# A mixer stage whose TensorE sequence is written by a timing model: other costs and rules in the model, and the other engines' order left to the framework's scheduler

## The chip, the core and the metric

The kernel runs on one NeuronCore of one Trainium2 chip. The metric is the device time of one execution in microseconds (us). TensorE (PE) multiplies matrices and writes to PSUM; VectorE (DVE) and ScalarE (ACT) do the elementwise work, GpSimd (POOL) a little more of it, and SyncE (SP) issues the loads. Each engine works through its own list of instructions in that list's order, and waits where an instruction needs what another engine has not finished.

## The reference, cut to what matters

One encoder layer: a feed-forward block (ffn), a mixer, a second ffn. All numbers are float32, with 512 tokens and 16 learned tokens ahead of them (T = 528), model width 1024.

```python
h = h + 0.5 * swiglu(rms_norm(h, ffn1_norm), ...)
u = rms_norm(h, mix_norm)
z = u @ w_in
zq_a, zi_a, zf_f, zf_b, zg_a, zq_b, zk_b, zv_b, zgate_a, zgate_b = split_cols(z, IN_SIZES)
y_a = hgrn2_bidir(zq_a, zi_a, zf_f, zf_b, zg_a, ...)    # 4 heads, a gated recurrence in both directions
y_b = axial_gqa(zq_b, zk_b, zv_b, ...)                  # 8 heads of softmax attention, 2 key heads
mixed = sigmoid(zgate_a) * (y_a @ w_up_a) + sigmoid(zgate_b) * (y_b @ w_up_b)
h = h + mixed @ w_out
h = h + 0.5 * swiglu(rms_norm(h, ffn2_norm), ...)
```

## The kernel before, in words

Every product of a weight with an activation is made of three matmuls, since both sides are cut into a high and a low part: whi with xh, whi with xl, wlo with xh. A weight block arrives in `raw` by DMA; ACT casts it to `whi`, DVE subtracts to get `wlo`. One block of 128 output rows is 8 slices of 3 matmuls; over 512 tokens each is one matmul of 512 columns, over 528 tokens it is one of 256 and one of 272.

The two ffns are scheduled by the framework and are not touched. The mixer is ordered by the program itself, in class `Order` (line 161 on). It holds a clock `t` for PE, times at which DVE and ACT come free, and a list of chains, each a Python generator with the time `ready` at which its next step could start. The main chain issues the weight products (`zcols`); after every slice of three matmuls `tick` calls `pump`, which runs the steps of all chains whose time has come. `account` charges each recorded instruction to the model: a matmul to `t`, a DVE or ACT instruction to that engine. `need` runs chains until a condition holds; where nothing is ready it moves `t` forward. `take` and `give` hand out the three PSUM banks named mm. So PE's list is what the model thinks will be ready when PE gets there. In the program before, a `manual_schedule` over ACT, DVE and POOL (line 699) binds these three to the order in which the model recorded their instructions too; PE is bound by an outer one (line 625).

The chains: `gla` (the recurrence of head hd) first makes a diagonal product, `gs<-zi,ks` on PE. Then come seven levels: ACT copies `ks` out of Z, PE makes four products `gs<-Z,ks`, DVE multiplies Z and tot (`grow`) and copies by mask from gs into A; an eighth product is `gs<-Z`. `gla_finish` transposes, makes the state (`vt,on`, `vt,st`) and the output (`vt,A`, `st,Z`), normalises it (ACT squares, twelve tiny DVE instructions in `newton`, ACT scales into `on`), and transposes on PE (`mm<-ident,on`). `scores` runs one attention tile at a time: four matmuls into S, a maximum on DVE (`nm`), `nr` and the exponential `pr` on ACT, a reciprocal `sm` on DVE, and a scaling of `pr` on ACT. `turned` transposes `pr` on PE (into at and am), ACT casts to `ph`, DVE subtracts to `pl`, and after four tiles PE multiplies with the values (`ph,vs`). There are 32 tiles in four groups j. The gates (`gate`, seven of them ahead of the attention's end, an eighth at c = 5) are weight products whose sigmoids ACT takes after the attention. Exp and sigmoid need different tables on ACT, and a change between them puts an ACT_TABLE_LOAD ahead.

`Timed` wraps the engines so that every recorded instruction carries the line of its one call, line 276; in the mixer, groups are told apart by their tiles.

Of the kernel before, what the change touches and what calls it, by code (L numbers as in the profile page):

```python
# [15 lines left out]
P = 128  # L16
D = 1024
KT = D // P
# [142 lines left out]
class Order:  # L161
# [12 lines left out]
    def account(self, eng, op, args, kw):  # L174
        out = kw.get("out", args[0])
        n, cur = 1, self.cur
        for d in out.shape[1:]:
            n *= d
        if eng == "pe":
            if cur is not self.main:  # L180
                self.t = max(self.t, cur.ready)
            if op == "transpose":
                self.t += 0.11
            elif args[1].dtype == F32R:
                self.t += n / 2400 + 0.0133
            else:
                self.t += max(4 * n / 2400, 0.06) + 0.005
            cur.ready, cur.eng = self.t + self.DRAIN, eng
            return
        if eng == "act":  # L190
            d = n * 0.000916 + 0.115
            if "accum_out" in kw:
                d += 0.19
            f = args[2] if len(args) > 2 else kw.get("func")
            if f in (AF.Exp, AF.Sigmoid, AF.Sqrt) and f != self.table:
                self.table = f
                d += 1.28
        elif op == "reciprocal":
            d = 0.0065 * n + 0.12
        elif op == "tensor_reduce":  # L200
            d = 0.70
        elif op == "memset":
            d = 0.15
        else:
            d = (n + 160) / 960
        start = max(self.free.get(eng, 0.0), cur.ready + (self.HOP if cur.eng != eng else 0.0))
        self.free[eng] = cur.ready = start + d
        cur.eng = eng
# [4 lines left out]
    def ready(self, ch):  # L213
        return ch.ready if ch.wait is None or ch.wait() else float("inf")

# [64 lines left out]
def block_kernel(tc, xT, wg1, wu1, wd1, w_in, wup, wout, wg2, wu2, wd2, params,  # L280
# [18 lines left out]
    with (tc.tile_pool(name="persist", bufs=1) as sp, tc.tile_pool(name="wts", bufs=1) as wp,  # L299
# [271 lines left out]
        with tc.tile_pool(name="f1", bufs=1) as ft:  # L571
# [45 lines left out]
            plan += tiles[:EARLY] + tiles[KT:KT + 5] + tiles[EARLY:KT] + tiles[KT + 5:]  # L617
            for c in range(KT):
# [6 lines left out]
        with tc.tile_pool(name="mix", bufs=1) as mp, tc.manual_schedule(engines={pe.engine}):  # L625
# [22 lines left out]
            def weights():  # L648
# [5 lines left out]
                if not W.ready:  # L654
# [42 lines left out]
            YA = []  # L697
            with (tc.tile_pool(name="heads", bufs=1) as hp, tc.tile_pool(name="small", bufs=1) as mn,
                  tc.manual_schedule(engines={act.engine, dve.engine, pool.engine})):
                Timed.clock = il  # L700
# [136 lines left out]

                waiting = []
                out_of = [0]

                def scores():

                    for j in range(HEADS):
# [3 lines left out]
                        for e in range(2):  # L847
                            for c in range(4):
# [27 lines left out]
                def turned():  # L876

                    for j in range(HEADS):
                        yb.append(mp.tile([P, SEQ], F32, name="yb", tag="yb", bufs=4))
                        for e in range(2):  # L880
# [3 lines left out]
                            for c in range(4):  # L884
                                yield lambda: waiting
                                _, _, _, pr, ready = waiting.pop(0)
                                il.cur.ready = max(il.cur.ready, ready)
# [16 lines left out]
                                yield  # L904
                            yield lambda: il.banks and out_of[0] < 3
                            av, v = mm(), VS[j // 2]
# [45 lines left out]
                def gla_inputs(hd):  # L952
# [5 lines left out]
                    scaled(Z[:, 3], zcols(SEQ))  # L958
                    yield
                    if hd:  # L960
# [3 lines left out]
                    yield  # L964
                    scaled(Z[:, 0], zcols(T))
                    yield
# [22 lines left out]
                def gla_head(hd, Z, tot, q, v):  # L989

                    A = hp.tile([P, 2, 4, P], F32, name="A", tag="A", bufs=2)
                    vt = hp.tile([P, 5, P], F32, name="vt", tag="vt", bufs=2)
                    ks = kbuf()
                    dve.tensor_tensor(ks, Z[:, 0, :SEQ], Z[:, 3, :SEQ], ALU.add)
                    first = il.cur.ready
                    o = four()
# [81 lines left out]
                def gla_out(hd, Z, tot, A, vt):  # L1078
# [59 lines left out]
                    give()  # L1138

                for gen in (prepare(), scores(), turned(), gla(), gla_finish()):  # L1140
                    il.add(gen)
                queries(0)
                gi = gla_inputs(0)
                kz, ksq = tmp("keys"), tmp("keys")
                scaled(kz, zcols(T))
# [14 lines left out]
                def gate(sg):  # L1160
                    (o, _), = zcols(SEQ)
                    dve.tensor_tensor(sg, o, R[:, :SEQ], ALU.mult)
                    give()

# [5 lines left out]

                sgs = []
                for c in range(EARLY):
                    sg = mp.tile([P, SEQ], F32, name="mixb", tag="mb", bufs=4) if c < 4 else tmp(f"b{c}")[:, :SEQ]
                    gate(sg)
                    sgs.append(sg)
# [3 lines left out]
                ybl = hp.tile([P, 4, SEQ], F32R, name="ybl", tag="pl")  # L1179
                for j, y in enumerate(yb):  # L1180
                    split((ybh[:, j, :], ybl[:, j, :]), y, slice(0, SEQ))
                    YB.append((ybh[:, j, :], ybl[:, j, :]))
                for sg in sgs:
                    act.activation(sg, sg, AF.Sigmoid)

                mixb = []
                for c in range(KT):
                    if c == 5:
                        sgs.append(tmp()[:, :SEQ])
                        gate(sgs[-1])  # L1190
                        act.activation(sgs[-1], sgs[-1], AF.Sigmoid)
# [117 lines left out]
```

## Time and profile before

| | us |
|---|---|
| time, median of 3 runs (lowest, highest) | 1239.66 (1239.02, 1242.03) |
| the profiled execution: its own time | 1241.96 |
| its span | 1240.1 |
| PE busy in the span | 1185.0 |
| DVE busy | 870.3 |
| ACT busy | 577.1 |
| POOL busy | 100.0 |

The stretch of the mixer that the change touches lies between about 381 and 752 us of the span. The page cuts the span into 40 slices of 31 us; PE falls below nine tenths in the first, the last, and slices 14 to 16 and 18 to 21 counted from 0, all in that stretch. A matmul in the trace lasts longer than the distance to the next one's start, since they are pipelined: a run of them costs its starts' distance.

### The profile page before, as it was taken

How to read it: one execution, taken by the hardware profiler on the slowest of the kernel's cores; microseconds unless marked ns; L12 is line 12 of the kernel's file. 1: busy time of each engine (PE TensorE's matmuls, PEld its weight loads, DVE VectorE, ACT ScalarE, POOL GpSimd, SP SyncE). 2: the span in 40 equal slices, each digit the busy share in tenths (PEclk: the TensorE clock that was granted, in tenths of full speed). 3: DMA queues.
4: the chain of work that ended last, by engine and by line, in shares of the span. 5: the costliest groups of instructions: out<-in, count | busy, mean ns of one | idle time of the engine just before them, and what ended most of it. 6: DMA issues, size and time to landing. Idle time of an engine off the chain costs nothing. (4 is left out here: it accounts for less than half of the span.)

```text
span 1240.1 us, 19340 instructions
## 1 busy us (share of the span) xinstructions
PE 1185.0 (96%) x7765; PEld 1077.0 (87%) x7765; DVE 870.3 (70%) x1409; ACT 577.1 (47%) x979; POOL 100.0 (8%) x77
## 2 busy tenths in 40 slices
PE   8999999999999987898888999999999999999998
PEld 8999999999998965786776887888888998998997
DVE  7988658748757786477686765545598875875863
ACT  5545435425554555545736424333454543543541
POOL 1011000001021000000000000112200201101100
PEclk8999999999999998899999999999999999999999
DMA  6233333322132210021020112323422423323213
GB/s 225 61 109 120 91 97 107 99 86 103 45 97 99 86 35 17 18 68 52 18 69 18 52 60 70 109 88 117 136 85 86 136 86 102 119 86 102 103 52 119
DMA packets 34233, 106.21 MB, mean 86 GB/s; under 512 B 3936, under 2 KB 4320, under 8 KB 34144
## 3 DMA queue, kind: packets, MB, share of 16 engines
q1 hardware_dynamic: 33984, 104.44, 26.1%
q8 instruction: 61, 1.00, 0.3%
q0 software_dynamic: 160, 0.54, 0.1%
q14 instruction: 28, 0.23, 0.1%
HBM read 102.87 MB, written 2.10 MB: 85 GB/s over the span
## 5 line engine op out<-in xcount | busy, mean ns | idle before, releaser
L101 ACT CAST whi<-raw 128x1024 fp32r<-128x1024 f32 (+2 forms) x179 | 150.0, 839 | 251.7 <-PE mm L294 88.6
L102 DVE TENSOR_TENSOR wlo<-raw,whi 128x1024 fp32r<-128x1024 f32 (+2 forms) x179 | 177.6, 995 | 20.6 <-ACT whi L101 18.6
L276 PE MATMUL mm<-xh,whi 128*128 128x512 f32 (+1 forms) x352 | 115.5, 365 | 0.0
L276 PE MATMUL mm<-xl,whi 128*128 128x512 f32 (+1 forms) x352 | 109.2, 348 | 0.0
L276 PE MATMUL mm<-xh,wlo 128*128 128x512 f32 (+1 forms) x352 | 109.0, 347 | 0.0
L102 DVE TENSOR_TENSOR wlo<-sums,whi 128x1024 fp32r<-128x1024 f32 x72 | 87.5, 1217 | 25.0 <-ACT whi L101 24.8
L101 ACT CAST whi<-sums 128x1024 fp32r<-128x1024 f32 x72 | 75.4, 1050 | 62.4 <-DVE sums L128 20.9
L133 POOL TENSOR_TENSOR sums<-raw 128x512 f32<-128x512 f32 x36 | 58.8, 1634 | 492.6 <-DVE wlo L102 483.4
L276 PEld LDWEIGHTS mm<-xh,wlo 128*128 128x128 f32 x352 | 62.3, 192 | 8.2
L276 PEld LDWEIGHTS mm<-xh,whi 128*128 128x128 f32 x352 | 62.9, 193 | 7.3 <-issue 0.7
L276 PEld LDWEIGHTS mm<-xl,whi 128*128 128x128 f32 x352 | 62.7, 193 | 5.4
L294 PE MATMUL mm<-hh,wlo 128*128 128x256 f32 (+1 forms) x218 | 63.0, 334 | 0.0
L294 PE MATMUL mm<-hh,whi 128*128 128x256 f32 (+1 forms) x218 | 62.8, 333 | 0.1
L294 PE MATMUL mm<-hl,whi 128*128 128x256 f32 (+1 forms) x218 | 62.9, 332 | 0.0
L471 PE MATMUL mm<-xl,whi 128*128 128x264 f32 (+1 forms) x216 | 61.3, 284 | 0.0
L471 PE MATMUL mm<-xh,whi 128*128 128x264 f32 (+1 forms) x216 | 61.2, 283 | 0.0
L471 PE MATMUL mm<-xh,wlo 128*128 128x264 f32 (+1 forms) x216 | 61.1, 283 | 0.0
L276 ACT CAST whi<-raw 128x1024 fp32r<-128x1024 f32 (+1 forms) x41 | 39.4, 965 | 36.9 <-PE mm L276 27.8
L294 PE MATMUL mm<-xh,whi 128*128 128x512 f32 (+2 forms) x152 | 51.4, 365 | 2.7 <-ACT xh L375 2.7
L276 DVE TENSOR_TENSOR wlo<-raw,whi 128x1024 fp32r<-128x1024 f32 (+1 forms) x41 | 45.8, 1116 | 9.8 <-ACT whi L276 9.6
L294 PE MATMUL mm<-xl,whi 128*128 128x512 f32 (+2 forms) x152 | 51.8, 367 | 0.0
L294 PE MATMUL mm<-xh,wlo 128*128 128x512 f32 (+2 forms) x152 | 51.2, 363 | 0.0
(351 smaller groups left out, 3574.3 us busy)
## 6 DMA issues: line engine op xcount, KB each, us to landing
raw<-in_wg SPq DMA_DIRECT2D x43, 512.0 KB, 3.9
raw<-in_wu SPq DMA_DIRECT2D x43, 512.0 KB, 3.3
raw<-in_w_in SPq DMA_DIRECT2D x42, 512.0 KB, 3.3
raw<-in_wd SPq DMA_DIRECT2D x48, 384.0 KB, 3.1
raw<-in_wd SPq DMA_DIRECT2D x16, 256.0 KB, 2.7
raw<-in_wup SPq DMA_DIRECT2D x16, 256.0 KB, 2.7
raw<-in_wout SPq DMA_DIRECT2D x8, 512.0 KB, 3.3
h<-in_xT SPq DMA_DIRECT2D x4, 528.0 KB, 6.7
```

Of the source, the lines that this page charges most:

```text
L101: nc.scalar.copy(hi[:, c], src)
L102: nc.vector.tensor_tensor(lo[:, c], src, hi[:, c].bitcast(F32), ALU.subtract)
L133: nc.gpsimd.tensor_tensor(t[:, E], r0[:, E], r1[:, E], ALU.add)
L276: return f(*args, **kw)
L294: pe.matmul(o, a[:, sl], b[:, cols], start=(k == 0 and i == 0), stop=(k == n - 1 and i == 2))
L471: pe.matmul(o, a[:, sl], b[:, kk, :], start=(start and kk == 0 and i == 0), stop=(kk == 3 and i == 2), skip_group_check=True)
```

## The change

The model: a chain's step on PE no longer waits for the drain of the chain's own PE step before it; an activation with `accum_out` costs 0.20 and not 0.19, one with a scale taken from a tile 0.17 more; a DVE `tensor_scalar` of over 64 columns costs (n + 160) / 1400 and not / 960. A condition may now give a time from which it holds, and `has_bank` gives the time at which a bank comes free; where the main chain wants a bank, other chains' steps due before that time are run first, and the clock moves with them.

The chains: the end of a softmax tile (reciprocal and scaling) is a chain of its own, so that `scores` goes on to the next tile; Z's forward gate is projected ahead of the query; two gates move into the loop over heads; the keys' squares take a buffer from `pr`'s set; the next weight's cast is recorded at once; sigmoids of the gates are recorded each behind its branch. The scheduling: ACT, DVE and POOL are no longer bound in the mixer. The framework's scheduler orders them by what it thinks is ready, with PE's list given.

```diff
         if eng == "pe":
-            if cur is not self.main:
+            if cur is not self.main and cur.eng != eng:
                 self.t = max(self.t, cur.ready)
...
             if "accum_out" in kw:
-                d += 0.19
+                d += 0.2
+            if not isinstance(kw.get("scale", 1.0), (int, float)):
+                d += 0.17
...
+        elif op == "tensor_scalar" and n > 64:
+            d = (n + 160) / 1400
         else:
             d = (n + 160) / 960
...
     def ready(self, ch):
-        return ch.ready if ch.wait is None or ch.wait() else float("inf")
+        w = True if ch.wait is None else ch.wait()
+        return max(ch.ready, 0.0 if w is True else w) if w else float("inf")
...
     def has_bank(self):
-        return bool(self.banks)
+
+        return self.banks and min(self.banks) + 1e-6
 
     def take(self):
 
         if self.cur is self.main:
-            self.need(self.has_bank)
+            while not self.banks or min(self.banks) > self.t:
+                ch = min(self.chains, key=self.ready, default=None)
+                r = self.ready(ch) if ch else float("inf")
+                if self.banks and min(self.banks) <= r:
+                    break
+                assert r < float("inf"), "nothing can go on"
+                self.t = max(self.t, r)
+                self.step(ch)
         r = min(self.banks)
...
-            order = [Z_QB, Z_KB, Z_FB, Z_VB, Z_QA, Z_FF, Z_G, Z_I]
+            order = [Z_QB, Z_KB, Z_FB, Z_VB, Z_FF, Z_QA, Z_G, Z_I]
             for hd in range(1, HEADS):
-                order += [c + hd for c in (Z_QB, Z_FB, Z_QA, Z_FF, Z_G, Z_I)]
+                order += [Z_GB + hd - 2] if hd > 1 else []
+                order += [c + hd for c in (Z_QB, Z_FB, Z_FF, Z_QA, Z_G, Z_I)]
...
-                    il.need(lambda: not W.ahead_raw)
+                    il.step(il.chains[-1])
                     W.fetch()
...
-            with (tc.tile_pool(name="heads", bufs=1) as hp, tc.tile_pool(name="small", bufs=1) as mn,
-                  tc.manual_schedule(engines={act.engine, dve.engine, pool.engine})):
+            with tc.tile_pool(name="heads", bufs=1) as hp, tc.tile_pool(name="small", bufs=1) as mn:
...
+                def scaled_rows(i, pr, sm):
+                    yield
+                    dve.reciprocal(sm, sm)
+                    yield
+                    act.activation(pr, pr, AF.Copy, scale=sm)
+                    pending[i] = pr, il.cur.ready
...
                                 act.activation(pr, s[:, WIDE], AF.Exp, bias=nr, scale=r, accum_out=sm)
-                                yield
-                                dve.reciprocal(sm, sm)
-                                yield
-                                act.activation(pr, pr, AF.Copy, scale=sm)
-                                waiting.append((j, e, c, pr, il.cur.ready))
+                                il.add(scaled_rows(len(pending), pr, sm))
+                                pending.append(None)
...
                 for hd in range(1, HEADS):
                     if hd > 1:
+                        early(hd - 2)
                         il.need(lambda: f"att{hd - 2}" in il.done)
...
-                for sg in sgs:
-                    act.activation(sg, sg, AF.Sigmoid)
...
                     b = branch(YB)
+                    act.activation(sgs[c], sgs[c], AF.Sigmoid)
```

The first place is on PE, behind the first head's output product. `ident,on` is the transposition of the normalised head; `at` and `am` are transpositions of a softmax tile, S the next tile's scores, `xh,whi` a weight product. Before:

```order
L276 MATMUL at<-ident,pr 128x128 x4
L276 MATMUL am<-ident,pr 16x128
L276 MATMUL mm<-xh,whi 128x256
L276 MATMUL mm<-xh,whi 128x272
L276 MATMUL mm<-xl,whi 128x256
L276 MATMUL mm<-xl,whi 128x272
L276 MATMUL mm<-xh,wlo 128x256
L276 MATMUL mm<-xh,wlo 128x272
L276 MATMUL mm<-ident,on 128x128 x4
```

A slice of weight product stood ahead of `ident,on`. Now, at the same place of PE's list:

```order
L289 MATMUL at<-ident,pr 128x128 x4
L289 MATMUL am<-ident,pr 16x128
L289 MATMUL S<-kh_4805,qst 128x256
L289 MATMUL S<-kh_4805,qst 128x272
L289 MATMUL S<-kl_4806,qst 128x256
L289 MATMUL S<-kl_4806,qst 128x272
L289 MATMUL mm<-ident,on 128x128 x4
L289 MATMUL mm<-kones,tq 128x2 x4
L289 MATMUL mm<-xh,whi 128x512
```

Four score matmuls stand directly ahead of it, and no weight product.

The second place is on ACT, at the start of the second group of attention tiles, with their exponentials `pr,sm<-S`. `mixb` is a gate's tile, and its row the sigmoid. The gates' sigmoids before, all behind the attention:

```order
L276 ACTIVATE on,ss<-mm 128x128 x4
L276 CAST ybh<-yb 128x512 x4
L276 ACTIVATE mixb<-mixb 128x512 x4
L276 ACTIVATE tm<-tm 128x512 x3
L276 ACTIVATE on<-mm,yo 128x128 x4
```

They stood together, with no table load between them. Now the first of them:

```order
L289 ACTIVATE pr<-pr,sm 128x528
L289 COPY vt<-gs 16x128
L289 ACT_TABLE_LOAD
L289 ACTIVATE mixb<-mixb 128x512
L289 COPY on<-mm 128x512
L289 ACTIVATE nr<-nm,yq 128x1
L289 COPY ks<-Z 128x512
L289 ACT_TABLE_LOAD
L289 ACTIVATE pr,sm<-S,nr,yq 128x528
L289 COPY st<-mm 128x128 x2
L289 ACTIVATE pr<-pr,sm 128x528
L289 CAST ph<-at 128x4x128
```

One sigmoid has moved between two exponentials and brought two table loads with it. Over the whole program ACT's list has 30 loads where it had 14.

The third place is on PE, in the second group of attention tiles: what stands between one tile's scores S and the transpositions of the tile ahead. Before:

```order
L276 MATMUL S<-kh_4766,qst 128x256
L276 MATMUL S<-kh_4766,qst 128x272
L276 MATMUL S<-kl_4767,qst 128x256
L276 MATMUL S<-kl_4767,qst 128x272
L276 MATMUL mm<-xh,whi 128x256
L276 MATMUL mm<-xh,whi 128x272
L276 MATMUL mm<-xl,whi 128x256
L276 MATMUL mm<-xl,whi 128x272
L276 MATMUL mm<-xh,wlo 128x256
L276 MATMUL mm<-xh,wlo 128x272
L276 MATMUL at<-ident,pr 128x128 x4
L276 MATMUL am<-ident,pr 16x128
```

Now the transpositions and the next scores, in the order of the list:

```order
L289 MATMUL at<-ident,pr 128x128 x4
L289 MATMUL am<-ident,pr 16x128
L289 MATMUL mm<-xh,whi 128x256
L289 MATMUL mm<-xh,whi 128x272
L289 MATMUL mm<-xl,whi 128x256
L289 MATMUL mm<-xl,whi 128x272
L289 MATMUL mm<-xh,wlo 128x256
L289 MATMUL mm<-xh,wlo 128x272
L289 MATMUL S<-kh_4805,qst 128x256
L289 MATMUL S<-kh_4805,qst 128x272
L289 MATMUL S<-kl_4806,qst 128x256
L289 MATMUL S<-kl_4806,qst 128x272
```

Six weight matmuls have moved from behind S to ahead of it, and behind this S stand 24 more weight matmuls, a level's product and one more slice until the next transpositions.

## Rows read from the trace of the kernel before

**Rows 1.** The page: the span, part 1's engines, and the granted clock of PE in 40 slices, in tenths.

```profile
span 1240.1 us, 19340 instructions
...
PE 1185.0 (96%) x7765; PEld 1077.0 (87%) x7765; DVE 870.3 (70%) x1409; ACT 577.1 (47%) x979; POOL 100.0 (8%) x77
...
PEclk8999999999999998899999999999999999999999
```

**Rows 2.** Busy time by stretch of the mixer: from the first to the last level product of a head, then on to the next head's first, for the four heads, and all of it. Columns: stretch, its length, then busy us and instructions of PE, PE's weight loads, DVE, ACT, POOL; PE's granted clock, DMA share, GB/s.

```profile
438.30:482.80 44.50, 32.47 (x181) 26.50 (x181) 37.15 (x72) 23.94 (x45) 0.00 (x0) 0.92 0.08 24
482.80:543.90 61.10, 53.19 (x305) 44.51 (x306) 31.98 (x67) 34.71 (x73) 0.18 (x2) 0.92 0.09 28
543.90:580.10 36.20, 31.30 (x194) 27.00 (x194) 31.28 (x58) 13.30 (x19) 0.00 (x0) 1.00 0.19 66
580.10:620.80 40.70, 34.59 (x221) 28.80 (x222) 25.38 (x57) 28.65 (x64) 0.44 (x2) 1.00 0.06 21
620.80:657.00 36.20, 31.24 (x194) 26.98 (x193) 31.29 (x58) 13.30 (x19) 0.00 (x0) 1.00 0.19 66
657.00:698.50 41.50, 35.97 (x221) 30.25 (x222) 25.47 (x57) 28.64 (x64) 0.42 (x1) 0.96 0.06 20
698.50:730.90 32.40, 32.24 (x171) 27.23 (x170) 24.81 (x35) 8.55 (x11) 0.00 (x0) 1.00 0.20 71
730.90:752.10 21.20, 20.05 (x112) 16.63 (x111) 9.99 (x25) 11.43 (x31) 0.00 (x0) 1.00 0.08 26
438.30:752.10 313.80, 271.06 (x1593) 227.88 (x1594) 217.34 (x426) 162.52 (x326) 1.04 (x5) 0.97 0.12 38
```

**Rows 3.** PE's waits between 420 and 800 us, the four longest in total: what waited, for which tile of which engine, us in total, times, the longest.

```profile
PE gs L276 <- DVE A L276: 17.1, 15, 3.7
PE at L276 <- DVE pl L276: 6.6, 6, 1.8
PE mm L276 <- ACT on L276: 4.0, 2, 2.0
PE at L276 <- ACT pr L276: 3.1, 6, 0.7
```

**Rows 4.** PE in order of time: start, length, instruction. The distance of two starts is what the first costs.

```profile
424.79 0.40 PE L276 MATMUL S<-kh,qst 128*128 128x256 f32 x2
...
425.28 0.40 PE L276 MATMUL mm<-xh,whi 128*128 128x256 f32 x2
...
431.12 0.39 PE L276 MATMUL mm<-xh,whi 128*128 128x512 f32 x1
431.35 0.39 PE L276 MATMUL mm<-xl,whi 128*128 128x512 f32 x1
...
435.48 0.60 PE L276 MATMUL at<-ident,pr 128*128 128x128 f32 x4
...
436.02 0.27 PE L276 MATMUL gs<-ident,tm 128*16 128x128 f32 x1
...
438.30 1.16 PE L276 MATMUL gs<-zi,ks 128*128 128x128 f32 x8 [0.62 <-ACT vt L276]
439.21 0.49 PE L276 MATMUL S<-kh,qst 128*128 128x256 f32 x2
```

**Rows 5.** PE in order of time: the scores of three attention tiles that follow one another.

```profile
492.60 0.75 PE L276 MATMUL S<-kh,qst 128*128 128x256 f32 x2
...
497.24 0.79 PE L276 MATMUL S<-kh,qst 128*128 128x256 f32 x2
...
502.44 0.49 PE L276 MATMUL S<-kh,qst 128*128 128x256 f32 x2
```

**Rows 6.** Groups of instructions of DVE and ACT between 400 and 780 us, shapes apart: count, busy us, mean ns of one, idle time before them.

```profile
L276 DVE TENSOR_REDUCE nm<-S 128x1 f32<-128x528 f32 x32 | 22.3, 698 | 1.0 <-PE S L276 0.7
L276 DVE TENSOR_TENSOR pl<-at,ph 128x512 fp32r<-128x512 f32 x32 | 22.0, 687 | 13.9 <-ACT ph L276 13.9
...
L276 DVE SCALAR_TENSOR_TENSOR ao<-ao,xo 128x4 f32<-128x4 f32 x12 | 2.0, 163 | 0.4
L276 DVE TENSOR_SCALAR Z<-Z,oml 128x512 f32<-128x512 f32 x4 | 1.9, 487 | 0.1
...
L276 ACT ACTIVATE pr<-pr,sm 128x528 f32<-128x528 f32 x32 | 23.6, 736 | 3.8 <-DVE sm L276 3.8
...
L276 ACT ACT_TABLE_LOAD x8 | 10.3, 1283 | 0.2
L276 ACT ACTIVATE nr<-nm,yq 128x1 f32<-128x1 f32 x32 | 9.5, 296 | 39.5 <-DVE nm L276 39.1
...
L276 ACT ACTIVATE on<-mm,yo 128x128 f32<-128x128 f32 x16 | 4.6, 370 | 4.2 <-DVE yo L276 4.2
...
L276 ACT ACTIVATE mixb<-mixb 128x512 f32<-128x512 f32 x4 | 2.2, 640 | 0.0
```

**Rows 7.** ACT in order of time around one table load, with the exponential behind it.

```profile
428.95 0.29 ACT L276 ACTIVATE nr<-nm,yq 128x1 f32<-128x1 f32 x1
429.26 1.28 ACT L276 ACT_TABLE_LOAD   x1
430.55 0.79 ACT L276 ACTIVATE pr<-S,nr,yq 128x528 f32<-128x528 f32 x1
```

**Rows 8.** Busy time by stretch, columns as in Rows 2: the 20 us in which the granted clock was lowest.

```profile
480.00:500.00 20.00, 16.96 (x86) 13.42 (x85) 10.36 (x21) 11.55 (x27) 0.00 (x0) 0.83 0.00 1
```

More of the change, by code (lines that the diff above doesn't have):

```diff
@@ L610, in last1 @@
                     rstd([(bank(g)[:, :c.stop - c.start], c) for g, c in zip(("gs", "at"), FULL)], T)
-            order = [Z_QB, Z_KB, Z_FB, Z_VB, Z_QA, Z_FF, Z_G, Z_I]
+            order = [Z_QB, Z_KB, Z_FB, Z_VB, Z_FF, Z_QA, Z_G, Z_I]
             for hd in range(1, HEADS):
-                order += [c + hd for c in (Z_QB, Z_FB, Z_QA, Z_FF, Z_G, Z_I)]
+                order += [Z_GB + hd - 2] if hd > 1 else []
+                order += [c + hd for c in (Z_QB, Z_FB, Z_FF, Z_QA, Z_G, Z_I)]
             plan = [w_in[c] for c in order]
             tiles = [w_in[Z_GB + c] for c in range(KT)] + [wup[c][:, 512:] for c in range(KT)]
-            plan += tiles[:EARLY] + tiles[KT:KT + 5] + tiles[EARLY:KT] + tiles[KT + 5:]
+            plan += tiles[HEADS - 2:EARLY] + tiles[KT:KT + 5] + tiles[EARLY:KT] + tiles[KT + 5:]
             for c in range(KT):
@@ L836, in prepare @@
                         yield from queries_rest(j, arg)
-                waiting = []
+                pending = []
                 out_of = [0]
+                def scaled_rows(i, pr, sm):
[4 more added lines that the diff above has]
+                    pending[i] = pr, il.cur.ready
                 def scores():
@@ L884, in turned @@
                             for c in range(4):
-                                yield lambda: waiting
-                                _, _, _, pr, ready = waiting.pop(0)
+                                i = (2 * j + e) * 4 + c
+                                yield lambda: len(pending) > i and pending[i] is not None
+                                pr, ready = pending[i]
                                 il.cur.ready = max(il.cur.ready, ready)
@@ L904, in turned @@
                                 yield
-                            yield lambda: il.banks and out_of[0] < 3
+                            yield lambda: out_of[0] < 3 and il.has_bank()
                             av, v = mm(), VS[j // 2]
@@ L959, in gla_inputs @@
                     yield
+                    scaled(Z[:, 0], zcols(T))
+                    yield
                     if hd:
@@ L963, in gla_inputs @@
                     scaled(zi[:, 0], zcols(SEQ))
-                    yield
-                    scaled(Z[:, 0], zcols(T))
                     yield
@@ L993, in gla_head @@
                     ks = kbuf()
+                    ready = il.cur.ready
                     dve.tensor_tensor(ks, Z[:, 0, :SEQ], Z[:, 3, :SEQ], ALU.add)
-                    first = il.cur.ready
+                    first, il.cur.ready = il.cur.ready, ready
+                    yield
                     o = four()
@@ L1138, in gla_out, with gate, early @@
                     give()
+                def gate(sg):
+                    (o, _), = zcols(SEQ)
+                    dve.tensor_tensor(sg, o, R[:, :SEQ], ALU.mult)
+                    give()
+                sgs = []
+                def early(c):
+                    sg = mp.tile([P, SEQ], F32, name="mixb", tag="mb", bufs=4) if c < 4 else tmp(f"b{c}")[:, :SEQ]
+                    gate(sg)
+                    sgs.append(sg)
                 for gen in (prepare(), scores(), turned(), gla(), gla_finish()):
@@ L1143, in block_kernel @@
                 gi = gla_inputs(0)
-                kz, ksq = tmp("keys"), tmp("keys")
+                kz, ksq = tmp("keys"), hp.tile([P, TP], F32, name="ksq", tag="pr", bufs=3)[:, :T]
                 scaled(kz, zcols(T))
@@ L1158, in block_kernel @@
                         pass
[L1160 to L1163, printed above, removed]
                 def branch(y):
@@ L1169, in branch @@
                     return b
[L1171 to L1175, printed above, removed]
+                for c in range(HEADS - 2, EARLY):
+                    early(c)
                 il.need(lambda: "attention" in il.done)
@@ L1179, in block_kernel @@
                 ybl = hp.tile([P, 4, SEQ], F32R, name="ybl", tag="pl")
+                ready = il.t
                 for j, y in enumerate(yb):
+                    il.main.ready = ready
                     split((ybh[:, j, :], ybl[:, j, :]), y, slice(0, SEQ))
                     YB.append((ybh[:, j, :], ybl[:, j, :]))
-                for sg in sgs:
-                    act.activation(sg, sg, AF.Sigmoid)
                 mixb = []
@@ L1190, in block_kernel @@
                         gate(sgs[-1])
-                        act.activation(sgs[-1], sgs[-1], AF.Sigmoid)
                     b = branch(YB)
+                    act.activation(sgs[c], sgs[c], AF.Sigmoid)
                     m = sgs[c] if c < 4 else mp.tile([P, SEQ], F32, name="mixb", tag="yb", bufs=4)
```

## The prediction

> **What bounds the kernel now.** I read the page first [rows 1]: PE is busy 1185.0 of 1240.1 us, so 55.1 us of PE are idle, and the granted clock is below nine tenths only in the first slice and in the middle of the span. Then the table by stretch [rows 2]. There the reader is to see three things. PE is idle for 313.8 - 271.06 = 42.7 us between 438.3 and 752.1. In the first head's levels, where DVE works 37.15 of 44.5 us, PE works least; in the fourth's, where attention is over, PE has 32.24 of 32.40. And in the levels of heads two and three DVE is busy 31.28 of 36.2 us, 86%, though it is DVE and its chain that hold PE there: 86% is as full as DVE gets. Third, PE's waits [rows 3]: 17.1 us are level products waiting for DVE's A, 6.6 and 3.1 us transpositions waiting for a softmax tile, 4.0 us the head's output. None of the four is for a DMA.
>
> Busy time hides a part of the loss, since a matmul behind a wait or at half clock shows as longer. So I count PE's list by the distance of starts [rows 4]: 0.23 us for a matmul of 512 columns, 0.24 for a pair of 256 and 272 (24 pairs from 425.28 to 431.12), 0.49 for a tile's four scores, 0.54 for a tile's five transpositions, 0.91 for a level's product. From the first head's `gs<-zi,ks` to the last `ident,on` the list of before has 447 weight matmuls of 512 columns (102.1 us at 0.2285), 288 halves (35.1), 30 tiles of scores (14.7) and 31 of transpositions (16.8), 36 level products (31.7 at 0.88), 72 matmuls of values (16.9, as long as weight matmuls), and 139 small ones (23.5, at 0.17 between a transposition's 0.11 and a level product's 0.22): 240.8 us. It took 313.8. The loss is 73.0 us, 42.7 of it shown as idle and the rest as slow clock and refilling. By the stretches of rows 2 the counted work is 25.0, 44.8, 28.6, 31.6, 28.6, 31.6, 31.0 and 19.8 us, so the losses are 19.5, 16.3, 7.6, 9.1, 7.6, 9.9, 1.4 and 1.4. A better placed list can give back that sum and no more; the ffns are untouched.
>
> **The change part by part.** *The costs.* The corrected costs meet the trace [rows 6]: `tensor_scalar` of 512 columns took 487 ns, where the model had (512 + 160) / 960 = 0.70 us and now has 0.48; the tiny `nr` took 296 ns, where it had 0.12 and now has 0.29; the scaling of `pr` took 736 ns, where it had 0.60 and now has 0.77. They lengthen a tile's chain in the model by 0.34 us; I give them nothing of their own, since they act through the list.
>
> *The list of PE.* It has 250.2 us of work from the first `gs<-zi,ks` to the last `ident,on`: all matmuls are as many as before, but the stretch now holds 36 more weight matmuls of 512 columns (8.2 us, gates and branch products that stood behind it) and one tile each more of scores and transpositions (1.0). What moves is the spacing. PE's work from the first to the last level product of a head was 25.0, 28.6, 28.6 and 31.0 us; it is now 49.0, 48.4, 42.7 and 39.2. The DVE work in such a run was 37 us in the first head and 31 in the next two [rows 2], that is 149% and 109% of PE's, and 80% in the fourth; the losses were 19.5, 7.6, 7.6 and 1.4. The same DVE work, 217 us and about 5 for what came in, now lies along 250 us of PE work, at 89%. Between 80% and 109% I read the loss off the straight line: 1.4 + 6.2 x 9/29 = 3.3 us for a run of 36 us, and there are seven such lengths in 250 us: 23 us. DVE alone bounds the stretch from below by 222 / 0.86 = 258 us, a loss of 8.
>
> Between the level runs PE lost 16.3, 9.1 and 9.9 us because attention tiles came one behind the other: their scores start 4.6 and 5.2 us apart [rows 5], which is the chain of maximum, `nr`, exponential, reciprocal, scaling and transposition with too little between them. Now the 31 tiles spread over all 250 us, one in 8, and a tile's tail no longer holds the next one's scores in the model. That removes this wait; what is late next is the queue of ACT and DVE.
>
> *What the scheduler's order adds.* Three kinds of place carry a wait that the model did not see. Directly ahead of the first head's `ident,on` stand a tile's scores. On DVE the twelve `newton` instructions of that head are now spread among others, and the last of them lie behind the maximum of just that tile; on ACT the scaling into `on` stands behind that tile's exponential and the scaling of the tile before. From the scores' end [rows 6]: maximum 0.70, `pl` 0.69, six tiny ones 1.1, the scaling of `pr` 0.74, the four scalings into `on` about 1.2 (they overlap; one is 0.37): 4.4 us less 0.3 that PE's four transpositions take, a wait of 4.1. Queued behind it on PE is everything else, a level product first. Two tiles' scores stand behind a table load: a copy of about 0.6 (an estimate from the sigmoid on as many columns, 0.64), the load 1.28 and the exponential 0.79 [rows 6, 7] make 2.7 us where PE has 1.6 and 1.3 of work: 2.5 us together. At the end the last tile's values follow its transposition at once: some 1 us. Sum 7.6; nothing, if a backlog elsewhere covers them.
>
> *Table loads.* ACT's list has 30 loads where it had 14: eight times a sigmoid now breaks a row of exponentials. At 1283 ns each [rows 6] that is 20.5 us more on ACT. ACT was busy 162.5 of 313.8 us [rows 2]; with the loads it is 183 of 282, 65%, and a tile's exponential has 8 us to happen in. I take them as hidden but for the two places above; if none is, 18 us more come on top. A load costs ACT its own length here: it starts 0.02 us after `nr` ends, and the exponential 0.01 us after the load [rows 7]. The Trainium skill (ScalarE: Activation LUTs, What ACT_TABLE_LOAD costs) states 1283 ns for the load, as rows 6 have it, and 1380 ns of drain with every switch, which rows 7 do not show. By that page sixteen switches would be 42.6 us on ACT, and with none hidden but the two above my sum would come out at 1239.
>
> *Weights and loads.* The next weights' cast and subtraction stay one block ahead, the loads on SP are as many and in nearly the same order, and no wait for `wlo` is among PE's longest [rows 3]. I cost them at nothing; the cover is one block of 24 x 0.23 = 5.5 us, and without it a block's cast and subtraction would be paid.
>
> The sum: 23 + 7.6 + 1.4 (the end as before) = 32 us lost where 73 were. The profiled execution took 1241.96 us, 1.9 more than its span: 1242.0 - 73.0 + 32.0 = 1201.0. It lies 2.3 us above the median of the runs, so I predict 1198.7, rounded 1199. The ends: a loss of 16 (DVE's floor of 8 and the places) gives 1183; a loss of 32 + 18, and 20 more for places that I priced at nothing, gives 1237.
>
> **The rivals.** *Smaller gain, the loads on the path.* The eight broken rows of exponentials delay a tile that PE's list wants at once. For it: the model gives a step to PE as soon as it thinks it ready, with a slice of 0.7 us as slack. Against it: one tile in 8 us, with a chain of 4.6. Price 18 to 38 us: 1217 to 1237.
>
> *The change doesn't do what it says: order against order.* PE's list is made by one model, the others' by a scheduler with another, and where the two differ a list waits as it did. The 4.1 us at `ident,on` are such a case. All of the 73 us would have to come back: 1240. Against it: of four `ident,on` only the first stands so.
>
> *Slower: ACT becomes the late engine.* The place is ACT's queue, where a pair of loads and a sigmoid (2 x 1.283 + 0.64 = 3.2 us) stand ahead of an exponential. If each of the eight stops PE in full, that is 26 us, and each stop may lower the clock: from 480 to 500 us the granted clock was 0.83 [rows 8], 17% of 20 = 3.4 us lost, eight times 27. With the 32 that makes 85 us, more than 73: 1242.0 - 73.0 + 85 - 2.3 = 1252. It decides once the losses pass 73, that is 41 us beyond my terms. If the Trainium skill's drain were paid as well, the losses would pass it sooner; the rows show no drain.
>
> *Larger gain.* If the straight line is too harsh and 89% on DVE costs as little as 80% did (1.4 us a run, 10 in all) and a backlog covers the places, 1242.0 - 73.0 + 11 - 2.3 = 1178.
>
> **How the numbers follow.** My forecast, 1185 to 1217: 0.58. Smaller gain, 1217 to 1236: 0.20. Larger, below 1185: 0.07. The same, 1236 to 1243: 0.05. Slower: 0.10. A measurement of this kernel can tell 0.3%, 3.7 us, from no change. So faster 0.84 (the first three, less 0.01 at the border), same 0.06, slower 0.10. The range 1183 to 1238 leaves out 0.06 below and 0.14 above; the likeliest case alone is 1185 to 1217.
>
> **What would show it.** In the changed profile PE's waits for A fall from 17.1 to under 8 us, those for `pl` and `pr` together from 9.7 to under 6, and PE's busy share passes 97%. The stretch from the first `gs<-zi,ks` to the last `ident,on` takes about 282 us, with the clock at 0.98 or more and DVE near 78%. One wait of 3 to 5 us for `on` stands in the first head. Table loads are 30, and ACT's busy time grows by 20 us. I am wrong if PE waits for `pr`, `ks` or S behind loads by more than 15 us in sum, or if the level products still wait for A as they did: then the spacing was not what lost the time.

## The result, and the profile after

The changed kernel took 1196.22 us (median of 4 runs, 1192.96 to 1199.43), the kernel before 1239.51 beside it: a ratio of 0.9647, 95% interval 0.9617 to 0.9676. The profiled execution took 1199.43 us, 1.8 more than its span. In the page, span, part 1 and the granted clock in 40 slices, as in [rows 1]:

```profile
span 1197.6 us, 19344 instructions
...
PE 1173.0 (98%) x7765; PEld 1074.6 (90%) x7765; DVE 860.5 (72%) x1409; ACT 596.9 (50%) x995; POOL 98.8 (8%) x77
...
PEclk9999999999999899989999999999999999999999
```

PE is busy 12 us less than before though it has the same 7765 matmuls, and idle 24.6 us where it was 55.1. ACT is busier by 19.8 us. Of that most is one group, here between 400 and 750 us (count, busy us, mean ns of one, idle before); it had 8 [rows 6]:

```profile
L289 ACT ACT_TABLE_LOAD x24 | 30.8, 1283 | 0.4
```

Next the stretches that answer to [rows 2]: the four runs of level products (first to last of a head), all from the first `gs<-zi,ks` to the last `ident,on`, and 6.8 us by themselves. Columns as there.

```profile
438.79:490.27 51.48, 51.48 (x333) 46.39 (x333) 45.95 (x89) 32.81 (x53) 0.11 (x1) 1.00 0.18 62
497.48:559.42 61.94, 55.39 (x338) 48.77 (x337) 44.18 (x93) 34.29 (x69) 0.11 (x1) 0.94 0.12 40
580.53:626.77 46.24, 45.98 (x288) 40.02 (x287) 41.78 (x91) 33.04 (x64) 0.00 (x0) 1.00 0.14 47
652.71:696.12 43.41, 41.95 (x243) 35.76 (x242) 34.55 (x66) 37.25 (x61) 0.00 (x0) 1.00 0.09 31
...
438.79:720.10 281.31, 269.11 (x1644) 233.89 (x1644) 214.44 (x436) 189.88 (x354) 0.73 (x5) 0.98 0.14 48
...
518.70:525.50 6.80, 6.58 (x25) 5.89 (x26) 3.76 (x10) 0.94 (x4) 0.00 (x0) 0.50 0.00 1
```

Where did the 1240.1 - 1197.6 = 42.5 us go? The stretch is 313.8 - 281.3 = 32.5 shorter, although by my count it holds 9.4 us more work (36 gate and branch matmuls, a tile). What lies behind it is 488.0 - 477.5 = 10.5 shorter, since that work has left it; what lies ahead is 0.5 longer. So the gain is PE time that was idle or slow in the mixer. In the first head's levels PE now has 333 matmuls and no idle time, where it had 181 in 44.5 us; the second head's run alone still loses much.

PE's waits between 380 and 790 us, as in [rows 3]:

```profile
PE mm L289 <- ACT on L289: 5.1, 1, 5.1
PE S L289 <- ACT pr L289: 4.2, 4, 2.1
PE mm L289 <- issue: 1.8, 1, 1.8
PE gs L289 <- ACT ks L289: 1.0, 1, 1.0
```

The 17.1 us of level products waiting for A are gone altogether. The largest wait left is a single one, for `on`. All engines in order of time show it, and ahead of it a table load (start, length, instruction, idle time before it and its releaser):

```profile
499.82 1.28 ACT L289 ACT_TABLE_LOAD   x1
...
501.12 0.79 ACT L289 ACTIVATE pr<-S,nr,yq 128x528 f32<-128x528 f32 x1
...
502.05 0.52 PE L289 MATMUL S<-kh,qst 128*128 128x256 f32 x2 [1.42 <-ACT pr L289]
...
511.86 0.16 DVE L289 TENSOR_SCALAR xo<-ss 128x4 f32<-128x4 f32 x1
...
513.06 1.25 DVE L289 TENSOR_TENSOR Z<-Z,tot 128x1056 f32<-128x1056 f32 x1
...
514.42 0.73 DVE L289 COPY_PREDICATED A<-msk,gs 128x512 f32<-128x512 uint8 x1
...
515.71 0.70 DVE L289 TENSOR_REDUCE nm<-S 128x1 f32<-128x528 f32 x1
...
516.39 0.68 DVE L289 TENSOR_TENSOR pl<-at,ph 128x512 fp32r<-128x512 f32 x1
...
517.77 0.16 DVE L289 SCALAR_TENSOR_TENSOR yo<-ao,yo 128x4 f32<-128x4 f32 x1
...
517.88 0.73 ACT L289 ACTIVATE pr<-pr,sm 128x528 f32<-128x528 f32 x1 [0.23 <-DVE sm L289]
518.52 1.12 ACT L289 ACTIVATE on<-mm,yo 128x128 f32<-128x128 f32 x4
518.92 1.25 PE L289 MATMUL mm<-ident,on 128*128 128x128 f32 x4 [5.13 <-ACT on L289]
```

`newton`'s twelve tiny instructions run from 511.86 to 517.93, 6.1 us, since the scheduler put Z, A, the maximum and `pl` among them (bound, in e2, they take 2.3); then ACT scales a softmax tile before it scales `on`. From 518.70 to 525.50 the granted clock stood at the lower of its two levels (0.50 above), behind a PE that had just stood still for 5.1 us: some 3.4 us more.

### The profile page after: what moved, and what is told of

The parts are those of the page before. It is cut to its first block, busy times and chain, and to the rows that moved or that the text cites. A ratio compares the mean times of both kernels' runs of the same rounds, so it can differ in the third digit from the quotient of the medians.

```text
span 1197.6 us, 19344 instructions
## 1 busy us (share of the span) xinstructions
PE 1173.0 (98%) x7765; PEld 1074.6 (90%) x7765; DVE 860.5 (72%) x1409; ACT 596.9 (50%) x995; POOL 98.8 (8%) x77
## 4 chain that ended last, share of the span: by engine, by line
PE 87%; DVE 5%; ACT 5%; DMA 2%; issue 1%; SPq 0%; POOL 0%; ACTq 0%; DVEq 0%
PE mm L307 20%; PE mm L289 19%; PE mm L484 14%; PE at L484 9%; PE at L307 5%; PE gs L484 4%; PE am L307 4%; PE S L307 4%; PE gs L289 2%; PE am L484 2%; DVE wlo L102 1%; ACT L289 1%; PE S L289 1%; ACT pr L289 1%; ACT whi L101 1%
## 5 line engine op out<-in xcount | busy, mean ns | idle before, releaser
L578 DVE SCALAR_TENSOR_TENSOR h<-mm,h 128x512 f32<-128x512 f32 (+2 forms) x40 | 20.9, 544 | 41.5 <-PE mm L307 41.5
```

Source lines behind the costliest of these rows:

```text
L578: dve.scalar_tensor_tensor(h[c][:, cols], o, 0.5, h[c][:, cols], ALU.mult, ALU.add)
```

## The experiments

Theory: TensorE's list, made by the mended model, carries the gain. Rivals: the scheduler's freedom carries it, or one cost alone. Each ratio is against the kernel before on the same chip.

| run | edit | us | ratio (95% interval) |
|---|---|---|---|
| changed kernel | | 1196.2 | 0.9647 (0.9617 to 0.9676) |
| e1 | before, ACT, DVE and POOL free | 1227.1 | 0.9883 (0.9868 to 0.9898) |
| e2 | changed, the three bound | 1192.8 | 0.9605 (0.9590 to 0.9620) |
| e3 | changed, all old costs | 1229.0 | 0.9908 (0.9882 to 0.9933) |
| e4 | changed, old bank rule | 1190.6 | 0.9584 (0.9569 to 0.9599) |
| e5 | changed, old ACT costs | 1195.7 | 0.9621 (0.9605 to 0.9638) |
| e6 | changed, old drain rule | 1229.3 | 0.9897 (0.9878 to 0.9916) |
| e7 | changed, old bank rule and bound | 1186.1 | 0.9548 (0.9530 to 0.9565) |
| e8 | changed, sigmoids left out | 1193.6 | 0.9613 (0.9592 to 0.9634) |
| e9 | before, drain rule mended alone | 1196.8 | 0.9633 (0.9611 to 0.9655) |
| e10 | changed, softmax end in one chain | 1218.7 | 0.9800 (0.9769 to 0.9831) |
| e11 | e7, free behind the attention | 1189.2 | 0.9568 (0.9546 to 0.9589) |
| e12 | e9 and the softmax end split | 1199.9 | 0.9659 (0.9643 to 0.9675) |

### The list or the freedom: e1 and e2

In e1 `manual_schedule` over ACT, DVE and POOL is removed from the kernel before:

```diff
-            with (tc.tile_pool(name="heads", bufs=1) as hp, tc.tile_pool(name="small", bufs=1) as mn,
-                  tc.manual_schedule(engines={act.engine, dve.engine, pool.engine})):
+            with tc.tile_pool(name="heads", bufs=1) as hp, tc.tile_pool(name="small", bufs=1) as mn:
```

> The kernel before with one edit: ACT, DVE and POOL are no longer bound in the mixer; TensorE's list is the old one, instruction for instruction. Theory (TensorE's list carries the gain, the freedom little): 1240, between 1228 and 1250, with level products still waiting 12 to 20 us for A or Z and the softmax waits (pl, pr) still 6 to 12 us. Rival (the gain is the scheduler's freedom on ACT and DVE): below 1210, with those waits under 5 us. Third view (freedom with a list not made for it hurts): above 1250.

It took 1227.1, 1.2% less than before: one us below my theory's lower end and far from the rival's 1210. PE's waits between 380 and 800 us in e1:

```profile
PE at L276 <- ACT pr L276: 8.9, 12, 1.8
PE mm L276 <- ACT on L276: 7.8, 3, 4.4
PE gs L276 <- DVE tot L276: 7.0, 6, 1.4
PE S L276 <- ACT pr L276: 5.2, 9, 1.4
PE gs L276 <- ACT ks L276: 3.5, 5, 1.3
...
PE gs L276 <- DVE A L276: 0.5, 2, 0.3
```

My expectation of the waits was wrong: the one for A fell from 17.1 to 0.5 us with PE's list unchanged. Part of it only changed its name: matmuls into gs now wait 7.0 us for DVE's `tot` and 3.5 for `ks`, 11.8 us in all where it was 20.9. The scheduler lets the levels through sooner, and the softmax tiles and `on` pay for part of it: the name that a wait carries is no proof of its cause. In e2 the same lines are put back into the changed kernel.

> The changed kernel with one edit: ACT, DVE and POOL are bound again to the recorded order in the mixer; TensorE's list is the changed one, instruction for instruction, and ACT has 16 table loads where the changed one has 30. Theory (the list carries the gain): 1188 to 1205; the 5.1 us wait for `on` in the first head falls to under 2 us, since newton then stands in the model's order. Rival (the scheduler's freedom carries it): above 1230, with DVE and ACT waits back on the levels.

It took 1192.8, within the theory's range. PE's longest wait there, and the one for `on`:

```profile
PE mm L289 <- DVE wlo L289: 2.1, 2, 1.3
...
PE mm L289 <- ACT on L289: 1.0, 2, 0.6
```

So the list is worth about 4% with the other engines bound (1 to 0.9605) and 2.4% with them free (0.9883 to 0.9647). Freedom gains 1.2% with the old list and, if anything, costs 0.4% with the new one (the intervals of e2 and the changed kernel just touch). The single wait for `on` was the scheduler's, as the prediction had it.

### Which of the costs: e3, e5 and e6

e3 undoes the edits of `account`, e5 those of ACT's durations alone, and e6 only this:

```diff
-            if cur is not self.main and cur.eng != eng:
+            if cur is not self.main:
                 self.t = max(self.t, cur.ready)
```

> The changed kernel with the old costs in the model (drain rule of a chain's TensorE steps, accum_out 0.19, no term for a scale from a tile, tensor_scalar over 960), all else as changed; ACT's list has 14 table loads. Theory (costs act by a few tenths of a us per tile; the list's spacing comes from the banks' rule and the chains): 1195 to 1210, softmax waits (pl, pr) 2 to 6 us more. Rival (the costs are what spaces the list): above 1222, with level products waiting 10 us or more again.

> The changed kernel without the model's terms for ACT (accum_out back at 0.19, no 0.17 for a scale from a tile); drain rule and tensor_scalar as changed; 30 table loads. With all costs old the time was 1229 and 18 scores waited 18.8 us for `pr`. Theory (the ACT terms are what was missing: nr and the exponential of a tile end 0.35 us later than the old model thinks, so S is placed too early): 1218 to 1232, scores waiting for `pr` over 12 us. Rival (the drain rule does it): within 5 us of the changed kernel, scores waiting under 6 us.

> The changed kernel with the old drain rule alone (a chain's TensorE step waits 0.3 us in the model for the chain's own TensorE step before it); ACT's terms as changed; 16 table loads. Theory (ACT's terms are what counts): 1190 to 1202, scores waiting for `pr` under 6 us. Rival (the drain rule is what counts): 1218 or more, with scores waiting over 12 us.

e3 took 1229.0, so the costs are most of the gain, against my theory. But its level products don't wait for A, as the rival had it; scores wait for the exponential that frees their bank. The line of e3:

```profile
PE S L285 <- ACT pr L285: 18.8, 18, 2.0
```

I took this for the missing ACT terms and was wrong again: without them (e5) the time is 1195.7, like the changed kernel's. The old drain rule alone (e6) gives 1229.3. Its first head's levels, busy time by stretch and then PE's longest wait:

```profile
437.86:478.00 40.14, 30.32 (x179) 25.51 (x178) 33.21 (x71) 25.32 (x49) 0.00 (x0) 0.91 0.06 19
```

```profile
PE S L289 <- ACT pr L289: 12.6, 12, 2.9
```

179 matmuls where the changed list has 333: this line of the model sets how much weight work the list puts between the steps of the chains. The reason can be counted in the code. `account` is called for every matmul, and each sets `cur.ready` to `t` plus 0.3 us; under the old rule the next matmul of the same step then moved the model's PE clock to that time. A step of k matmuls was charged (k - 1) x 0.3 us too much: 3 for a tile's scores, 4 for its transpositions, 2 for its share of the values' product, nine in 32 tiles make 288; 3 for each of 36 level products, 108; 26 a head for the other steps of the recurrence (3 + 3 + 4 + 13 + 3), 104; and 15 in preparing queries, keys and values. 515 x 0.3 = 154.5 us. The trace has no such gap: a tile's four score matmuls cost 0.49 us [rows 4], and the rule charged 0.9 on top. The Trainium skill (TensorE: Matmul & The Clock Gate, Step-by-step: what each phase is for) says that a matmul's drain overlaps the fill of the next; the starts 0.23 us apart in [rows 4], for matmuls that last 0.39, agree. To a model whose PE is that slow, every chain looks ready after fewer weight matmuls than it really needs.

### Is that line enough: e9 and e12

e9 makes that one edit in the kernel before; all else, the binding too, is as before.

```diff
-            if cur is not self.main:
+            if cur is not self.main and cur.eng != eng:
                 self.t = max(self.t, cur.ready)
```

> The kernel before with one condition edited: in the model, a chain's matmul no longer waits 0.3 us for the drain of the matmul that the same step recorded just before it (515 matmuls in the mixer paid it, 154.5 us of the model's TensorE clock); all else as before, ACT, DVE and POOL bound. Theory (this rule set the old model's clock far behind the chip's and is the largest part, but the chains must be able to use it): 1212 to 1228; level products wait under 6 us for A. Rival 1 (the rule is all of it): under 1202. Rival 2 (without the other parts it gives nothing): 1236 or more.

1196.8: rival 1. One condition gives a ratio of 0.9633, which can't be told from the whole change. In e9, the first head's levels and the whole stretch by busy time, then all of PE's waits above 1.5 us and the one for A:

```profile
443.88:484.76 40.88, 40.61 (x267) 36.26 (x266) 36.72 (x66) 24.09 (x39) 0.11 (x1) 1.00 0.17 57
...
443.88:691.80 247.92, 241.28 (x1517) 212.10 (x1517) 203.39 (x405) 151.79 (x305) 0.75 (x5) 0.98 0.14 46
```

```profile
PE mm L276 <- ACT on L276: 3.6, 4, 2.6
PE mm L276 <- ACT whi L276: 2.6, 1, 2.6
PE mm L276 <- issue: 2.2, 1, 2.2
PE gs L276 <- ACT vt L276: 1.8, 1, 1.8
...
PE gs L276 <- DVE A L276: 0.2, 1, 0.2
```

267 matmuls between the first head's first and last level product instead of 181 [rows 2], and PE busy in 40.6 of 40.9 us. e12 adds the split of the softmax tile's end:

```diff
-                                yield
-                                dve.reciprocal(sm, sm)
-                                yield
-                                act.activation(pr, pr, AF.Copy, scale=sm)
-                                waiting.append((j, e, c, pr, il.cur.ready))
+                                il.add(scaled_rows(len(pending), pr, sm))
+                                pending.append(None)
```

> The kernel before with two edits: the mended drain rule (alone 1196.8) and the softmax tile's end as a chain of its own; ACT, DVE and POOL bound. Theory (the split counts only in the changed kernel's list; here no scores wait for `pr` as it is): 1192 to 1201, level with the drain rule alone. Rival (the split is worth its 20 us wherever the drain rule is mended, as far as TensorE has idle time left): under 1190. Third view (a list that the model spaces worse): over 1204.

1199.9: the split adds nothing there.

### The other parts: e4, e7, e10, e11

e10 undoes that split in the changed kernel. e4 restores the old bank rule:

```diff
-            while not self.banks or min(self.banks) > self.t:
-                ch = min(self.chains, key=self.ready, default=None)
...
+            self.need(self.has_bank)
```

e7 restores it and binds the three engines; e11 is e7 with the binding ended where the attention ends.

> The changed kernel with one part undone: reciprocal and scaling of a softmax tile are again steps of the chain that makes the scores, so that the next tile's scores come behind them in the model; the costs, the bank rule and the freedom as changed. Theory (the split is the second large part, since a tile's chain of 4.6 us otherwise bounds 32 tiles one behind the other): 1208 to 1222. Rival (with the drain rule mended the order comes out as well): within 5 us of the changed kernel.

> The changed kernel with the old rule for PSUM banks (a bank is free once it is given back, the main chain waits for it by moving its clock, no other chain's step is run first), all else as changed. Theory: the banks' rule is one of two equal parts of the spacing, 1200 to 1215, with short waits of weight matmuls for DVE's eviction of a bank (tm, Z) of 3 to 8 us more. Rival (the rule changes nothing that TensorE waits for): within 4 us of the changed kernel, 1192 to 1200.

> The changed kernel with two of its parts undone at once: the old bank rule (alone 1190.6) and ACT, DVE and POOL bound to the recorded order (alone 1192.8); 16 table loads. Theory (the two gains have one cause, the 5.1 us wait for `on` with the half clock behind it, so they don't add): 1187 to 1193, level with the old bank rule alone. Rival (they add): 1183 to 1186.

> The changed kernel with the old bank rule and with ACT, DVE and POOL bound to the recorded order until the attention's end only, free behind it; 28 table loads. The version bound throughout took 1186.05 and waited 1.2 us for ybh and ybl and 2.1 us for wlo behind the attention's end. Theory (those waits go, the loads are hidden): 1181 to 1186. Rival (the loads that come back stand ahead of exponentials and cost as much): 1187 to 1193.

e10 took 1218.7, as expected: in the changed list the split is worth some 19 us (0.9800 against 0.9647), though e9 reaches the changed kernel's time without it. That tiles come one behind the other is not what its trace shows: PE waits 2.7 + 1.8 = 4.5 us for `pr` there and 4.2 in the changed kernel. PE is idle for 35.5 us of the span where it was 24.6, the longest waits being for `on`, and the granted clock is 0.982 where it was 0.991; what the split holds up in this list stays open. PE's waits in e10:

```profile
PE mm L289 <- ACT on L289: 8.3, 3, 3.8
...
PE at L289 <- ACT pr L289: 2.7, 2, 2.5
...
PE S L289 <- ACT pr L289: 1.8, 1, 1.8
```

The parts lean on each other; undoing one part tells what it holds up, not what it adds. e4 came out below both views, at 1190.6: its interval lies clear of the changed kernel's, so the new bank rule costs some 0.6%. By busy time, e4's stretch from the first `gs<-zi,ks` to the last `ident,on`:

```profile
434.58:707.90 273.32, 265.66 (x1650) 231.44 (x1649) 213.40 (x437) 188.46 (x353) 0.74 (x5) 0.99 0.15 49
```

Against the changed kernel's 281.31 that is 8.0 us less. The two profiled executions lie at opposite ends of their kernels' spreads (1187.85 in 1187.85 to 1191.84, and 1199.43 in 1192.96 to 1199.43), so this tells the kind of loss and not its size. Idle time is 4.5 less (7.7 where there were 12.2; the wait for `on` is 2.6 where it was 5.1). Slow clock is about 5 less, one stretch of 3.4 us at the lower level (514.35 to 517.76) where the changed kernel has three, 13.6 us together; that is 1.6 more than the difference, and e4's stretch has six more matmuls in the trace. Why the new rule spaces the list worse isn't settled.

e7 is the fastest of all, 1186.1 or a ratio of 0.9548: between the two ranges. By ratios the gains add nearly in full, as the rival had it: 0.0042 of e2 and 0.0063 of e4 make 0.0105, and it gained 0.0099. So the wait for `on` can't be the whole of both, though e4 shortens it too. PE's longest waits in it:

```profile
PE mm L281 <- DVE wlo L281: 2.1, 2, 1.3
PE mm L281 <- issue: 1.5, 1, 1.5
PE mm L281 <- ACT ybh L281: 1.0, 1, 1.0
```

e11 was to remove the first and third. It did, but with ACT free at the end the sigmoids moved up into the row of exponentials (28 loads for 16), and two scores waited for `pr`:

```profile
PE S L281 <- ACT pr L281: 3.8, 2, 2.6
```

1189.2, the rival's range; the intervals of e7 and e11 overlap, so it gains nothing that can be told.

### The table loads: e8

In e8 the sigmoids of the eight gates are left out, with a copy in their place:

```diff
-                    act.activation(sgs[c], sgs[c], AF.Sigmoid)
+                    act.activation(sgs[c], sgs[c], AF.Copy)
```

> The changed kernel with the sigmoids of the eight gates of branch B left out (a copy in their place, so that the output is not that of the reference); TensorE's list is the same and ACT has 18 table loads where the changed kernel has 30, 12 x 1.283 = 15.4 us less on ACT. Theory (the loads are hidden but for two places of 2.5 us together): 1192 to 1197. Rival (loads on the path in full): 1179 to 1184. If the waits for `pr` ahead of S (1.4 and 2.1 us) stay, they were not the loads' doing.

1193.6, in the theory's range. Twelve loads less are 15.4 us less on ACT, and the ratio moves by 0.0034, some 4 us, within the intervals. The wait for `on` is still there, and PE's waits of scores for `pr` in e8 are:

```profile
PE S L289 <- ACT pr L289: 2.3, 2, 2.1
```

The wait of 1.42 us behind the gate's load is gone; the one of 2.1 stays. By my expectation a wait that stays is not the loads' doing; that doesn't follow here, since e8 leaves the load ahead of this one in place. In the changed kernel:

```profile
558.81 1.09 ACT L289 ACTIVATE Z<-Z 128x1056 f32<-128x1056 f32 x1
...
560.57 1.28 ACT L289 ACT_TABLE_LOAD   x1
...
562.80 0.60 PE L289 MATMUL S<-kh,qst 128*128 128x256 f32 x2 [2.09 <-ACT pr L289]
...
564.06 1.08 ACT L289 ACTIVATE Z<-zi 128x1056 f32<-128x1056 f32 x1
```

The scheduler has put an exponential between the recurrence's two sigmoids, `Z<-Z` and `Z<-zi`, with a table load on either side of it. In the kernel before the two follow each other (532.70 and 533.69 us) behind one load, and in e2 they do so again (555.12 and 556.11), with 16 loads where e8 has 18.

## Why the prediction was right, and where it was not

The time was right: 1199 was predicted, 1196.2 measured; for the profiled execution 1201.0 and 1199.4. Point by point:

**The loss.** The stretch was to take 282 us and took 281.3; with 250.2 us of counted work the loss is 31.1 where I had 32. The signs that I named are there too: PE 98% busy, the clock at 0.98, DVE 76% (I had 78), 16 table loads more and 19.8 us more on ACT, one long wait for `on` in the first head, none for A.

**The term of 23 us for DVE's load** came right in its sum by luck. By the step "Between 80% and 109% I read the loss off the straight line" every run of levels should lose 3.3 us in 36, so 4.5, 4.4, 3.9 and 3.6. The runs lost 51.48 - 49.0 = 2.5, 61.94 - 48.4 = 13.5, 46.24 - 42.7 = 3.5 and 43.41 - 39.2 = 4.2. No wait for A is left to carry such a term, and the first run's 2.5 us were lost with PE never idle at full clock: my count of work is short by some 5% there. In all, 12.2 us were idle, 6.8 were slow clock (half of the three stretches of 13.6 us), and 12 are in neither; 5% of 250.2 us is 12.5, an estimate by which that shortness can be all of it. So what met the 23 us is, as far as the rows tell, in good part work that I had not counted. Nor is 86% "as full as DVE gets", from which I took the floor of 258 us: DVE was busy 45.95 of 51.48 us in the changed kernel's first run, 89%, and 36.72 of 40.88 in e9's, 90%.

**The wait for `on`** was sized at 4.1 and measured 5.13; it lay where I had put it, for the reason that I gave, and e2 takes it away by binding. What I left out of the sum is the slow clock behind it, 3.4 us, which I had priced only in the slower rival. That one place is most of the 13.5.

**The table loads** were taken as hidden but for two places of 2.5 us. There are two such places, 1.42 and 2.09 us, 3.5 in sum, and for the gates' loads e8 bears out that the rest is hidden. At the first place the exponential starts at 501.12, 0.02 us after its load ends. The Trainium skill (ScalarE: Activation LUTs, What ACT_TABLE_LOAD costs) adds 1380 ns of drain to each switch; the rows after show none, as [rows 7] did not.

**The costs** are the step that failed: "They lengthen a tile's chain in the model by 0.34 us; I give them nothing of their own, since they act through the list." I worked out the durations, which e5 shows to matter little, and never priced the drain rule, which I had read as one wait per step. It is charged per matmul, and undone (e6, 0.9897) it takes back seven tenths of the gain; alone (e9) it gives all of it. What e6 keeps, 1.0%, is no more than the freedom alone gave the old list in e1. The spacing of the list was the right quantity, read off the order of instructions; what made the spacing I had wrong.

**The softmax tail.** "That removes this wait" isn't shown: without the split the changed list is 19 us slower (e10), but not by PE's waits for softmax tiles, and in e9's list those are down to 0.3 us without it.

**The scheduler.** The freedom in the change's title carries none of the gain: bound again, the kernel is no slower (e2). The rival "order against order" is true in the small, for one place, and the rivals that put the loads or ACT on the path, from 1217 us on, never came near.

**Not priced at all:** the bank rule. It has no term in the sum, and it costs about 0.6% (e4; e7 against e2).

## What to carry to other kernels

Where a timing model writes an engine's list, compare the model's clock with the trace before refining its durations: one term charged per instruction instead of per step outweighed all other edits here, and it can be found by counting calls. Test the smallest edit alone on the old kernel as well as undone in the new one, since parts that look necessary in one may do nothing in the other. And a free scheduler may repair a bad list (1.2% in e1) without being of use to a good one.

## What the runs showed of the hardware

A stop of PE could cost more than its length. In the changed kernel PE stood 5.13 us and then ran 6.8 us at the 1.2 GHz level (0.50 between 518.70 and 525.50); the run of levels in which it lies has 0.94 where the first head's, with no stop, has 1.00. After the stop of 2.09 us at 562.80 there is such a stretch too, of 3.4 us, and after the one of 1.42 at 502.05 there is none until 518.70. The length alone doesn't decide it: in e2 a stop of 1.41 us, up to 607.16, was followed by 3.4 us at the lower level, and in the changed kernel the clock was low from 699.60 to 703.02 behind four stops in the 10 us before, the longest of 0.98 us. Busy time by stretch, two of the changed kernel and then that of e2:

```profile
502.05:518.70 16.65, 11.74 (x75) 10.26 (x75) 12.72 (x30) 10.62 (x28) 0.11 (x1) 1.00 0.10 32
563.07:566.49 3.42, 3.42 (x17) 3.42 (x17) 2.18 (x6) 3.17 (x4) 0.11 (x1) 0.50 0.00 0
```

```profile
607.41:610.81 3.40, 3.40 (x15) 3.00 (x15) 2.97 (x6) 0.00 (x0) 0.00 (x0) 0.50 0.41 148
```
